# Add-and-normalise with 4 MB transfers, two rings of rows, a store lag of 48 rows, and one row in eight added on VectorE

## The chip, the core and the metric

The kernel runs on one core of one Trainium2 chip; the other cores are idle. The metric is the device time of one execution in microseconds (us). Runs of one kernel mostly agree within 0.3%. Each kernel was timed in alternating rounds with the kernel before on the same chip. A run is called fast or slow by its time and by the granted TensorE clock. "Span" is the time inside the profile, about 1.9 us shorter than the device time of the same run.

The engines are TensorE (PE in the profile; PEld is its weight load), VectorE (DVE), ScalarE (ACT) and SyncE (SP), which here only issues DMA transfers. Sixteen DMA engines move the data; every large transfer of this kernel is spread over all sixteen (sixteen landings each in the trace).

## The reference

```python
# x, residual: 16 x 1024 x 512 float32
z = x + residual
mean = np.mean(z, axis=-1, keepdims=True)
var = np.var(z, axis=-1, keepdims=True)
out = gamma * (z - mean) / np.sqrt(var + eps) + beta
```

There are 16,384 rows of 512 numbers. On 128 partitions that is 128 rows per partition, and "row" from here on means one such slice: 128 x 512 numbers, 0.26 MB. For each row the kernel loads x and the residual and stores the result, 0.79 MB; in all it moves 100.67 MB.

## The kernel before

SyncE alone issues all large transfers, in program order: the loads of a chunk, then the store of the chunk five behind.

```python
CHUNKS = [2, 2, 4] + [8] * 14 + [4, 2, 2]      # rows per chunk; 8 rows = 2 MB, 16 KB per partition
GROUP = 4                                      # rows per compute step
STORE_LAG = 5; Z_BUFS = 7; R_BUFS = 4          # in chunks

def load(c):
    z = zpool.tile(...); r = rpool.tile(...)
    nc.sync.dma_start(out=z[...], in_=rows(xf, c))
    nc.sync.dma_start(out=r[...], in_=rows(rf, c))

def g_add(g):                                  # z + r on TensorE, by an identity matrix
    for j in ...:
        nc.tensor.matmul(ps, ident, Z[c][:, j, :], start=True, stop=False)
        nc.tensor.matmul(ps, ident, R[c][:, j, :], start=False, stop=True)

# ScalarE: z <- ps with the row sum; later Square(z - mean) with its sum; sqrt
# VectorE: negmean; affine1: z <- (z - mean) * gamma; affine2: z <- z * rstd + beta
# a group's last step (affine2) comes three steps after its add

for k in range(n_chunks + STORE_LAG):
    if k < n_chunks:
        load(k)
    ...
    c = k - STORE_LAG
    if c >= 0:
        while done <= c:
            done = next(steps)
        store(c)
```

With seven z buffers and a lag of five, the x load of chunk k reuses the buffer of chunk k-7. The store of that chunk was issued after load k-2, so the loads of chunk k-1 and the store of chunk k-6 (6.3 MB) are queued between the store and the load that must wait for it.

## Time and profile before

The median is 251.63 us (251.4 to 251.81). What matters:

| Reading | Value | View |
|---|---|---|
| TensorE busy | 226.2 us, never idle from 10 to 220 us | engine totals, slices |
| VectorE, ScalarE busy | 182.7 us, 180.4 us | engine totals |
| DMA rate in steady state | 427 to 429 GB/s | windows |
| TensorE per row | 1.72 us (four matmul instructions 0.43 us apart) | timeline |
| Chain of waits | 88% TensorE | chain |

From the page of the kernel before: the engine totals, four rows of the picture in 40 slices (digits are tenths busy), and the chain of work that ended last.

```profile
PE 226.2 (91%) x516; PEld 99.2 (40%) x516; DVE 182.7 (73%) x328; ACT 180.4 (72%) x548; POOL 0.7 (0%) x6
...
PE   5999999999999999999999999999999999997000
...
DVE  1121266888888888898888888888988888889993
...
DMA  6999999999999999999999999999999999987087
GB/s 245 421 440 428 425 429 379 438 427 425 436 430 430 429 433 425 428 433 433 428 428 430 425 433 425 433 425 433 428 432 427 428 430 416 427 353 299 42 357 315
...
PE 88%; DVE 8%; DMA 1%; issue 1%; ACT 0%; DVEq 0%
```

TensorE and the DMA engines are both full until 220 us: a tuned balance. The chain names only one of them. At the end there is a hole: a slice of 42 GB/s between two of 299 and 357.

The same by windows: start and end of the window, its length, busy time of each engine, then the granted clock, the busy share of the DMA engines, and GB/s.

```profile
20.00:120.00 100.00, 100.00 (x234) 44.19 (x233) 72.27 (x129) 78.53 (x242) 0.00 (x0) 1.00 1.01 427
120.00:220.00 100.00, 100.00 (x234) 44.27 (x233) 82.59 (x148) 81.27 (x252) 0.00 (x0) 1.00 1.01 429
223.00:227.00 4.00, 4.00 (x11) 1.72 (x10) 3.77 (x8) 4.00 (x14) 0.00 (x0) 1.00 0.19 82
...
232.00:238.00 6.00, 0.00 (x0) 0.00 (x0) 5.96 (x12) 2.98 (x10) 0.00 (x0) 0.63 0.00 0
```

In the last two windows all loads are in, and the next store waits for VectorE.

Now SyncE's timeline (start, duration, line, transfer). L66 loads x, L69 the residual, L77 stores.

```profile
84.07 0.33 SPq L66 DMA_DIRECT2D z<-in_x_dram  x1
84.45 0.47 SPq L69 DMA_DIRECT2D r<-in_residual_dram  x1
88.91 0.34 SPq L77 DMA_DIRECT2D out_dram<-z  x1
98.64 0.33 SPq L66 DMA_DIRECT2D z<-in_x_dram  x1
```

The x load at 98.64 us waited for a store issued at 75.18 us. By then a load pair and another store (84.07 to 88.91) were already queued, so the DMA engines went on working. The wait list of SyncE:

```profile
SPq L66 <- DMA out_dram<-z: 135.9, 13, 13.3
```

It waited 135.9 us in 13 waits.

### The profile page before, as it was taken

The page shows a single profiled execution, that of the slowest core. Times are in us where ns is not written, and L with a number is a line of the kernel's source. Part 1 is how long each engine was busy: PE and PEld are TensorE (multiplying, and loading weights), DVE is VectorE, ACT ScalarE, POOL GpSimd, SP SyncE. Part 2 cuts the span into 40 slices and gives each one's busy share as a digit, 9 for nine tenths or more (in the row PEclk, how much of TensorE's full clock was granted, in tenths as well). Part 3 has the DMA queues.
Part 4 walks back from the last instruction along what each step waited for, and adds up shares of the span by engine and source line. Part 5 has one row for each costly group of instructions (what it writes and reads, how often), then busy time and mean ns, then how long its engine had stood idle before and what let it go on. Part 6 is the DMA issues. An engine that isn't in the chain of part 4 may idle for free.

```text
span 249.7 us, 2117 instructions
## 1 busy us (share of the span) xinstructions
PE 226.2 (91%) x516; PEld 99.2 (40%) x516; DVE 182.7 (73%) x328; ACT 180.4 (72%) x548; POOL 0.7 (0%) x6
## 2 busy tenths in 40 slices
PE   5999999999999999999999999999999999997000
PEld 1444444444444444444444444444444444442000
DVE  1121266888888888898888888888988888889993
ACT  2157578888777777788887777777888877779600
POOL 1000000000000000000000000000000000000000
PEclk9999999999999999999999999999999999999755
DMA  6999999999999999999999999999999999987087
GB/s 245 421 440 428 425 429 379 438 427 425 436 430 430 429 433 425 428 433 433 428 428 430 425 433 425 433 425 433 428 432 427 428 430 416 427 353 299 42 357 315
DMA packets 8656, 100.80 MB, mean 404 GB/s; under 512 B 962, under 2 KB 962, under 8 KB 2500
## 3 DMA queue, kind: packets, MB, share of 16 engines
q1 hardware_dynamic: 8640, 100.67, 95.4%
q8 instruction: 4, 0.07, 0.1%
q14 instruction: 8, 0.07, 0.1%
q10 hardware_dynamic: 4, 0.00, 0.0%
HBM read 67.11 MB, written 33.55 MB: 403 GB/s over the span
## 4 chain that ended last, share of the span: by engine, by line
PE 88%; DVE 8%; DMA 1%; issue 1%; ACT 0%; DVEq 0%
PE ps L112 43%; PE ps L113 43%; DVE z L191 5%; DVE z L176 3%; PE ps L98 1%; DMA gb_row<-in_gamma_dram 1%; ACT z L121 0%; DVEq L267 0%; DVE rstd L188 0%; DVE nm L163 0%
## 5 line engine op out<-in xcount | busy, mean ns | idle before, releaser
L112 PE MATMUL ps<-z,ident 128*128 128x512 f32 x256 | 132.4, 599 | 0.0
L113 PE MATMUL ps<-r,ident 128*128 128x512 f32 x256 | 131.7, 596 | 0.0
L121 ACT ACTIVATE z<-ps 128x512 f32<-128x512 f32 x128 | 75.4, 589 | 50.2 <-PE ps L113 50.2
L139 ACT ACTIVATE junk<-z,nm 128x512 f32<-128x512 f32 x128 | 90.5, 711 | 1.4 <-DVE nm L163 1.4
L191 DVE SCALAR_TENSOR_TENSOR z<-z,rstd,beta_t 128x512 f32<-128x512 f32 x128 | 87.8, 747 | 1.2
L176 DVE SCALAR_TENSOR_TENSOR z<-z,nm,gamma_t 128x512 f32<-128x512 f32 x128 | 87.7, 745 | 1.1 <-ACT junk L139 1.1
L112 PEld LDWEIGHTS ps<-z,ident 128*128 128x128 f32 x256 | 49.1, 192 | 62.8 <-issue 48.7
L113 PEld LDWEIGHTS ps<-r,ident 128*128 128x128 f32 x256 | 49.0, 192 | 62.3 <-issue 61.7
L163 DVE TENSOR_SCALAR nm<-sm 128x4 f32<-128x4 f32 (+1 forms) x34 | 5.8, 170 | 54.9 <-ACT z L121 54.9
L121 ACT ACTIVATION_READ_ACCUMULATOR z<-ps 128x1 f32 x128 | 24.9, 195 | 0.0
L139 ACT ACTIVATION_READ_ACCUMULATOR junk<-z,nm 128x1 f32 x128 | 24.4, 191 | 0.0
L151 ACT ACTIVATE std<-ssq,eps_t 128x4 f32<-128x4 f32 (+1 forms) x34 | 9.8, 289 | 0.1
L98 PE MATMUL ps<-gb_row,ones 1*128 1x512 f32 x4 | 3.7, 1085 | 3.1 <-DMA gb_row<-in_gamma_dram 3.1
L188 DVE RECIPROCAL rstd<-std 128x4 f32<-128x4 f32 (+1 forms) x34 | 5.8, 170 | 0.0
L121 ACT ACT_TABLE_LOAD x1 | 1.3, 1283 | 4.3 <-DMA z<-in_x_dram 4.3
L99 DVE COPY gamma_t<-ps 128x512 f32<-128x512 f32 x1 | 0.7, 692 | 4.2 <-PE ps L98 4.2
L98 PEld LDWEIGHTS ps<-gb_row,ones 1*128 1x128 f32 x4 | 1.1, 307 | 4.2 <-issue 3.3
L99 DVE COPY beta_t<-ps 128x512 f32<-128x512 f32 x1 | 0.7, 692 | 1.0 <-PE ps L98 1.0
L151 ACT ACT_TABLE_LOAD x1 | 1.3, 1283 | 0.0
L87 DVE MEMSET ones<- 1x128 f32 x1 | 0.2, 165 | 0.8 <-PEq L253 0.8
masks.py:199 POOL TENSOR_SCALAR_AFFINE_SELECT ident<-ident 128x128 f32<-128x128 f32 x1 | 0.3, 295 | 0.1
masks.py:197 POOL MEMSET ident<- 128x128 f32 x1 | 0.2, 205 | 0.3 <-POOLq L253 0.3
(5 smaller groups left out, 0.5 us busy)
## 6 DMA issues: line engine op xcount, KB each, us to landing
z<-in_x_dram SPq DMA_DIRECT2D x14, 2048.0 KB, 19.4
r<-in_residual_dram SPq DMA_DIRECT2D x14, 2048.0 KB, 23.9
out_dram<-z SPq DMA_DIRECT2D x14, 2048.0 KB, 26.6
z<-in_x_dram SPq DMA_DIRECT2D x4, 512.0 KB, 7.4
r<-in_residual_dram SPq DMA_DIRECT2D x4, 512.0 KB, 8.2
z<-in_x_dram SPq DMA_DIRECT2D x2, 1024.0 KB, 9.0
r<-in_residual_dram SPq DMA_DIRECT2D x2, 1024.0 KB, 15.0
out_dram<-z SPq DMA_DIRECT2D x4, 512.0 KB, 8.3
```

Of the source, the lines that this page charges most:

```text
L87: nc.vector.memset(ones, 1.0)
L98: nc.tensor.matmul(ps, ones, gb_row[:, k, :], start=True, stop=True)
L99: nc.vector.tensor_copy(dest, ps)
L112: nc.tensor.matmul(ps, ident, Z[c][:, j, :], start=True, stop=False)
L113: nc.tensor.matmul(ps, ident, R[c][:, j, :], start=False, stop=True)
L121: nc.scalar.activation(out=Z[c][:, j0 + k, :], in_=PS[g_copy][k], func=ACT.Identity, accum_out=sm[:, k : k + 1],)
L139: nc.scalar.activation(out=junk, in_=Z[c][:, j0 + k, :], func=ACT.Square, bias=NM[g_square][:, k : k + 1], accum_out=ssq[:, k : k + 1],)
L151: nc.scalar.activation(out=std[:, :n], in_=SSQ.pop(g)[:, :n], func=ACT.Sqrt, bias=eps_t[:, 0:1], scale=inv_d,)
L163: nc.vector.tensor_scalar(out=nm[:, :n], in0=NM[g][:, :n], scalar1=-inv_d, scalar2=None, op0=ALU.mult,)
L176: nc.vector.scalar_tensor_tensor(out=zj, in0=zj, scalar=NM[g][:, k : k + 1], in1=gamma_t, op0=ALU.add, op1=ALU.mult,)
L188: nc.vector.reciprocal(out=rstd[:, :n], in_=STD.pop(g)[:, :n])
L191: nc.vector.scalar_tensor_tensor(out=zj, in0=zj, scalar=rstd[:, k : k + 1], in1=beta_t, op0=ALU.mult, op1=ALU.add,)
```

## The change

Its intent: fewer, larger transfers; a deep backlog of stores, so that DMA has work while the last rows are computed; and less work on TensorE. The diff cut to its core:

```diff
-CHUNKS = [2, 2, 4] + [8] * 14 + [4, 2, 2]
+CHUNKS = [8, 8] + [16] * 6 + [8, 8]
-STORE_LAG = 5
-Z_BUFS = 7
-R_BUFS = 4
+Z_ROWS = 64
+R_ROWS = 32
+STORE_LAG = 48
+ADD_PERIOD = 8
...
+    zbuf = consts.tile([P, Z_ROWS, D], FP32)       # ring: row j lives at j % Z_ROWS
+    rbuf = consts.tile([P, R_ROWS, D], FP32)
     def load(c):
+        nc.sync.dma_start(out=part(zbuf, Z_ROWS, c), in_=rows(xf, c))
+        nc.sync.dma_start(out=part(rbuf, R_ROWS, c), in_=rows(rf, c))
...
+    def on_vector(j):
+        return j % ADD_PERIOD == ADD_PERIOD - 1
+    def add_on_vector(g): ...                      # z <- z + r with its row sum, on VectorE
...
+    for c in range(n_chunks + 1):
+        asked = end[c] if c < n_chunks else N // P + STORE_LAG
+        if c < n_chunks:
+            while added < asked - R_ROWS: ...      # residual rows must have been added
+            load(c)
+        while stored < n_chunks and end[stored] <= asked - STORE_LAG:
+            while done < end[stored]: ...
+            store(stored)
+            stored += 1
```

More of the change, by code (lines that the diff above doesn't have):

```diff
@@ L41 @@
     assert N == P * sum(CHUNKS)
-    NJ = max(CHUNKS)
-    starts = [P * sum(CHUNKS[:c]) for c in range(len(CHUNKS))]
+    first = [sum(CHUNKS[:c]) for c in range(len(CHUNKS))]
     def rows(t, c):
-        return t[starts[c] : starts[c] + P * CHUNKS[c], :].rearrange(
-            "(p j) d -> p (j d)", p=P
-        )
+        lo = P * first[c]
+        return t[lo : lo + P * CHUNKS[c], :].rearrange("(p j) d -> p (j d)", p=P)
     consts = ctx.enter_context(tc.tile_pool(name="consts", bufs=1))
-    zpool = ctx.enter_context(tc.tile_pool(name="zpool", bufs=Z_BUFS))
-    rpool = ctx.enter_context(tc.tile_pool(name="rpool", bufs=R_BUFS))
     small = ctx.enter_context(tc.tile_pool(name="small", bufs=6))
@@ L58, with part, zrow, rrow @@
     ctx.enter_context(tc.manual_schedule())
-    Z, R = {}, {}
-    def load(c):
-        n = CHUNKS[c]
-        z = zpool.tile([P, NJ, D], FP32, tag="z", name="z")
-        r = rpool.tile([P, NJ, D], FP32, tag="r", name="r")
-        nc.sync.dma_start(
-            out=z[:, :n, :].rearrange("p a b -> p (a b)"), in_=rows(xf, c)
-        )
-        nc.sync.dma_start(
-            out=r[:, :n, :].rearrange("p a b -> p (a b)"), in_=rows(rf, c)
-        )
-        Z[c], R[c] = z, r
-    def store(c):
-        n = CHUNKS[c]
-        z = Z.pop(c)
-        nc.sync.dma_start(
-            out=rows(of, c), in_=z[:, :n, :].rearrange("p a b -> p (a b)")
-        )
+    zbuf = consts.tile([P, Z_ROWS, D], FP32)
+    rbuf = consts.tile([P, R_ROWS, D], FP32)
+    def part(buf, size, c):
+        lo = first[c] % size
+        assert lo + CHUNKS[c] <= size
+        return buf[:, lo : lo + CHUNKS[c], :].rearrange("p a b -> p (a b)")
+    def load(c):
+        nc.sync.dma_start(out=part(zbuf, Z_ROWS, c), in_=rows(xf, c))
+        nc.sync.dma_start(out=part(rbuf, R_ROWS, c), in_=rows(rf, c))
+    def store(c):
+        nc.sync.dma_start(out=rows(of, c), in_=part(zbuf, Z_ROWS, c))
+    def zrow(j):
+        return zbuf[:, j % Z_ROWS, :]
+    def rrow(j):
+        return rbuf[:, j % R_ROWS, :]
+    def on_vector(j):
+        return j % ADD_PERIOD == ADD_PERIOD - 1
     gb_row = consts.tile([1, 2, D], FP32)
@@ L103, with add @@
         for j in range(0, n, GROUP):
-            groups.append((c, j, min(GROUP, n - j)))
-    PS, NM, SSQ, STD = {}, {}, {}, {}
-    def g_add(g):
-        c, j0, n = groups[g]
-        PS[g] = []
+            groups.append((first[c] + j, min(GROUP, n - j)))
+    n_groups = len(groups)
+    PS, SM, NM, SSQ, STD = {}, {}, {}, {}, {}
+    def add(g):
+        j0, n = groups[g]
+        SM[g] = small.tile([P, GROUP], FP32, tag="sm", name="sm")
         for j in range(j0, j0 + n):
+            if on_vector(j):
+                continue
@@ L111, in g_add @@
             ps = psum.tile([P, D], FP32, tag="ps", name="ps")
-            nc.tensor.matmul(ps, ident, Z[c][:, j, :], start=True, stop=False)
-            nc.tensor.matmul(ps, ident, R[c][:, j, :], start=False, stop=True)
-            PS[g].append(ps)
-    def act_step(g_copy, g_square, g_sqrt):
-        if g_copy is not None:
-            c, j0, n = groups[g_copy]
-            sm = small.tile([P, GROUP], FP32, tag="sm", name="sm")
-            for k in range(n):
+            nc.tensor.matmul(ps, ident, zrow(j), start=True, stop=False)
@@ new lines, in add, with add_on_vector @@
+            nc.tensor.matmul(ps, ident, rrow(j), start=False, stop=True)
+            PS[j] = ps
+    def add_on_vector(g):
+        j0, n = groups[g]
+        for j in range(j0, j0 + n):
+            if on_vector(j):
+                nc.vector.scalar_tensor_tensor(
+                    out=zrow(j),
+                    in0=zrow(j),
+                    scalar=0.0,
+                    in1=rrow(j),
+                    op0=ALU.add,
+                    op1=ALU.add,
+                    accum_out=SM[g][:, j - j0 : j - j0 + 1],
+                )
@@ L121, in act_step, with copy @@
+    def copy(g):
+        j0, n = groups[g]
+        for j in range(j0, j0 + n):
+            if j in PS:
                 nc.scalar.activation(
-                    out=Z[c][:, j0 + k, :],
-                    in_=PS[g_copy][k],
+                    out=zrow(j),
+                    in_=PS.pop(j),
                     func=ACT.Identity,
-                    accum_out=sm[:, k : k + 1],
+                    accum_out=SM[g][:, j - j0 : j - j0 + 1],
                 )
-                if k == 0 and g_sqrt is not None:
-                    sqrt(g_sqrt)
-                    g_sqrt = None
@@ L130, in act_step, with negmean @@
-            NM[g_copy] = sm
-            PS.pop(g_copy)
-        if g_sqrt is not None:
-            sqrt(g_sqrt)
-        if g_square is not None:
-            c, j0, n = groups[g_square]
-            ssq = small.tile([P, GROUP], FP32, tag="ssq", name="ssq")
-            for k in range(n):
-                junk = junkp.tile([P, D], FP32, tag="junk", name="junk")
-                nc.scalar.activation(
-                    out=junk,
-                    in_=Z[c][:, j0 + k, :],
-                    func=ACT.Square,
-                    bias=NM[g_square][:, k : k + 1],
-                    accum_out=ssq[:, k : k + 1],
-                )
-            SSQ[g_square] = ssq
+    def negmean(g):
+        n = groups[g][1]
+        nm = small.tile([P, GROUP], FP32, tag="nm", name="nm")
+        nc.vector.tensor_scalar(
+            out=nm[:, :n],
+            in0=SM.pop(g)[:, :n],
+            scalar1=-inv_d,
+            scalar2=None,
+            op0=ALU.mult,
+        )
+        NM[g] = nm
@@ L148, in sqrt, with square @@
+    def square(g):
+        j0, n = groups[g]
+        ssq = small.tile([P, GROUP], FP32, tag="ssq", name="ssq")
+        for k in range(n):
+            junk = junkp.tile([P, D], FP32, tag="junk", name="junk")
+            nc.scalar.activation(
+                out=junk,
+                in_=zrow(j0 + k),
+                func=ACT.Square,
+                bias=NM[g][:, k : k + 1],
+                accum_out=ssq[:, k : k + 1],
+            )
+        SSQ[g] = ssq
     def sqrt(g):
-        n = groups[g][2]
+        n = groups[g][1]
@@ L158, in sqrt @@
         STD[g] = std
-    def negmean(g):
-        n = groups[g][2]
-        nm = small.tile([P, GROUP], FP32, tag="nm", name="nm")
-        nc.vector.tensor_scalar(
-            out=nm[:, :n],
-            in0=NM[g][:, :n],
-            scalar1=-inv_d,
-            scalar2=None,
-            op0=ALU.mult,
-        )
-        NM[g] = nm
     def affine1(g):
-        c, j0, n = groups[g]
+        j0, n = groups[g]
         for k in range(n):
-            zj = Z[c][:, j0 + k, :]
             nc.vector.scalar_tensor_tensor(
-                out=zj,
-                in0=zj,
+                out=zrow(j0 + k),
+                in0=zrow(j0 + k),
                 scalar=NM[g][:, k : k + 1],
@@ L183, in affine1 @@
             )
+        NM.pop(g)
     def affine2(g):
-        c, j0, n = groups[g]
+        j0, n = groups[g]
         rstd = small.tile([P, GROUP], FP32, tag="rstd", name="rstd")
@@ L189, in affine2 @@
         for k in range(n):
-            zj = Z[c][:, j0 + k, :]
             nc.vector.scalar_tensor_tensor(
-                out=zj,
-                in0=zj,
+                out=zrow(j0 + k),
+                in0=zrow(j0 + k),
                 scalar=rstd[:, k : k + 1],
@@ L198, in affine2 @@
             )
-        NM.pop(g)
-    n_groups = len(groups)
-    def ok(g):
-        return g if 0 <= g < n_groups else None
     def compute_steps():
-        done = 0
-        for t in range(n_groups + 3):
-            if ok(t) is not None:
-                g_add(t)
-            act_step(ok(t), ok(t - 1), ok(t - 2))
-            if ok(t - 2) is not None:
-                affine1(t - 2)
-            if ok(t) is not None:
-                negmean(t)
-            if ok(t - 3) is not None:
-                affine2(t - 3)
-                c, j0, n = groups[t - 3]
-                if j0 + n == CHUNKS[c]:
-                    done = c + 1
-            yield done
+        stages = [
+            (0, add),
+            (0, add_on_vector),
+            (0, copy),
+            (2, sqrt),
+            (1, square),
+            (2, affine1),
+            (0, negmean),
+            (3, affine2),
+        ]
+        added = done = 0
+        for t in range(n_groups + 3):
+            for lag, stage in stages:
+                if 0 <= t - lag < n_groups:
+                    stage(t - lag)
+            if t < n_groups:
+                added += groups[t][1]
+            if t >= 3:
+                done += groups[t - 3][1]
+            yield added, done
     steps = compute_steps()
-    done = 0
+    added = done = stored = 0
     n_chunks = len(CHUNKS)
-    for k in range(n_chunks + STORE_LAG):
-        if k < n_chunks:
-            load(k)
-        if k == 0:
-            spread()
-        c = k - STORE_LAG
-        if c >= 0:
-            while done <= c:
-                done = next(steps)
-            store(c)
+    end = [first[c] + CHUNKS[c] for c in range(n_chunks)]
+    for c in range(n_chunks + 1):
+        asked = end[c] if c < n_chunks else N // P + STORE_LAG
+        if c < n_chunks:
+            while added < asked - R_ROWS:
+                added, done = next(steps)
+            assert stored == n_chunks or first[stored] >= asked - Z_ROWS
+            load(c)
+        if c == 0:
+            spread()
+        while stored < n_chunks and end[stored] <= asked - STORE_LAG:
+            while done < end[stored]:
+                added, done = next(steps)
+            store(stored)
+            stored += 1
 _INS = ['x', 'residual', 'gamma', 'beta', 'eps']
```

## The prediction

> **What bounds the kernel now.** Two things, so evenly that neither waits in steady state. Table by stage (20 us stretches from 20 to 220 us): the 16 DMA engines are busy all the time and move 416 to 431 GB/s; the kernel must move 100.67 MB, so about 234 us at 430. That is near the 435 GB/s ceiling in the Trainium skill ("DMA: Bandwidth & Descriptors", Specifications). TensorE is busy in every one of these stretches as well: 226 us of 250, matmul starts 0.43 us apart, 4 per row, 1.72 us a row; the chain of waits lies 86% on it.
>
> DMA's loss beyond 234 us is at the ends. Start: no bytes before 1.6 us, then 307 to 389 GB/s until 8 us with the small chunks. End: stores wait for compute: the 40 slices show 353, 299, 42, 357, 315 GB/s, and SyncE waits 29 us for VectorE after 220 us. Against 430 GB/s that is about 11 us lost.
>
> **What the change does.**
> 1. One row in eight leaves TensorE: 1.72 x 7/8 = 1.50 us a row. VectorE gets 16 more passes of about 0.75 us: 183 to about 195 us, also 1.5 a row. Compute can now keep ahead of DMA (1.83 us a row at 430 GB/s).
> 2. Stores 48 rows behind: when the last load lands, about 12.6 MB of stores (29 us) remain, enough to cover the last rows' compute. The 11 us hole at the end should go.
> 3. 16 and 32 KB lines from the start: about 1 us at the start and at most 1 to 1.5 us in steady state, as 430 is near the ceiling.
> 4. New cost: z ring 64 rows minus lag 48 leaves 16 rows, exactly one chunk. In SyncE's order the x loads of chunks 5, 6, 7 and 8 each wait for completion of the store issued immediately before them, with nothing queued behind. DMA runs dry four times. Before, 6 MB always lay in between. Estimated cost of a hole: about 0.6 us from the last byte to the semaphore (end of the profile), 0.9 us from issue to the first packet and about 0.5 us ramp (start of the profile) = 2.0 us; the skill's fixed cost of about 2 us per DMA ("DMA: Bandwidth & Descriptors", Anatomy of one DMA) agrees. Four holes: 8 us, plus 0.8 us for unequal engines (the drain at 223 to 226 us shows up to 3 us of skew).
>
> **Sum.** Start 2.1 + transfer 233.1 + holes 8.8 + end 1.4 = 245.4 us span; plus 1.9 us (time over span before) = 247.3 us. The holes give back most of the tail's gain.
>
> **What would show each step.** DMA about 430 GB/s up to the end including a store-only last 30 us; four dips of about 2 us in fine windows (near 90, 121, 154 and 186 us), each ended by an x load; SyncE's wait "x load on store" remaining, its last waits on VectorE nearly gone; TensorE near 200 us busy; the chain of waits moving from TensorE to DMA.
>
> **What would make it wrong.** Holes nearer 1 us, or 32 KB lines giving 435: about 243. Holes over 3 us, slower store-only or load-only streams, or the residual load of chunk 4 waiting for TensorE (I find only about 4 us slack): 250 or more.
>
> Predicted 247.3 us, 8 in 10 between 244.3 and 250.6; faster by over 2%: 0.36, within 2%: 0.60, slower: 0.04.

## The result, and the profile after

The changed kernel is correct and slower: median 261.99 us (261.9 to 262.05) against 251.63. The ratio is 1.041, 95% interval 1.039 to 1.043. (A ratio is the mean time of one kernel's fast runs over that of the other's of the same rounds, so it is not quite the ratio of the medians.)

The same lines of the page as before:

```profile
PE 207.9 (80%) x452; PEld 89.3 (34%) x452; DVE 191.0 (73%) x356; ACT 169.9 (65%) x514; POOL 0.7 (0%) x6
...
PE   3699996999999999998998069993699999990000
...
DVE  1101438399999999999799803999319999999980
...
DMA  7999999999999869999399997899959999999957
GB/s 257 431 441 463 423 408 473 407 418 449 418 433 405 376 247 408 466 332 463 106 409 460 342 433 272 363 463 403 390 257 332 433 433 400 418 451 423 410 249 322
...
DMA 49%; PE 37%; DVE 8%; SPq 1%; issue 1%; ACT 0%; DVEq 0%
```

TensorE was relieved as intended (226.2 to 207.9 us busy), and the chain moved from TensorE to DMA. But four slices now fall to 247, 106, 272 and 257 GB/s, and TensorE has gaps of its own behind them.

SyncE's timeline (here L69 loads x, L70 the residual, L73 stores) shows a new pattern: each x load is preceded by silence, and nothing is queued between the store and the load.

```profile
92.76 0.34 SPq L69 DMA_DIRECT2D zbuf<-in_x_dram  x1
93.20 0.37 SPq L70 DMA_DIRECT2D rbuf<-in_residual_dram  x1
93.62 0.42 SPq L73 DMA_DIRECT2D out_dram<-zbuf  x1
127.78 0.33 SPq L69 DMA_DIRECT2D zbuf<-in_x_dram  x1
```

The load at 127.78 us overwrites the rows of the store issued at 93.62 us. Ring (64) minus lag (48) leaves 16 rows, which is one chunk. The total of this wait is smaller than before, and yet here it costs:

```profile
SPq L69 <- DMA out_dram<-zbuf: 121.9, 4, 33.7
```

The windows around the four x loads, columns as before:

```profile
90.00:94.00 4.00, 4.00 (x11) 1.76 (x10) 3.96 (x10) 3.69 (x14) 0.00 (x0) 1.00 0.46 133
124.00:129.00 5.00, 5.00 (x13) 2.17 (x12) 3.85 (x9) 4.61 (x14) 0.00 (x0) 1.00 0.32 92
159.00:163.00 4.00, 4.00 (x11) 1.77 (x10) 2.32 (x6) 3.08 (x10) 0.00 (x0) 1.00 0.46 131
193.00:197.00 4.00, 4.00 (x11) 1.77 (x10) 2.96 (x7) 3.72 (x12) 0.00 (x0) 1.00 0.39 82
```

One cycle, from one x load to the next, moves 12.58 MB: 24 packets of 32 KB for each DMA engine. A packet takes 1.213 us when nothing disturbs it, so 24 take 29.1 us. The cycles took 35.0, 33.6 and 33.5 us:

```profile
92.76:127.78 35.02, 33.57 (x79) 14.70 (x78) 32.64 (x62) 28.78 (x88) 0.00 (x0) 1.00 0.89 360
127.78:161.38 33.60, 24.27 (x53) 10.44 (x52) 21.67 (x42) 19.04 (x60) 0.00 (x0) 0.85 0.92 375
161.38:194.92 33.54, 27.16 (x58) 11.69 (x57) 23.79 (x45) 21.15 (x67) 0.00 (x0) 0.90 0.92 376
```

So a dry spell costs 4.4 to 5.9 us and not the 2.2 us that the prediction had put on it (2.0, and a quarter of 0.8 for unequal engines). The semaphore and packet records of the trace show why (landings of the store on the 16 engines, issue of the x load that waits for it):

```
store lands on its first .. last engine   spread   x load issued
 90.60 ..  92.70                           2.10       92.76
124.70 .. 127.77                           3.07      127.78
159.74 .. 161.36                           1.62      161.38
193.33 .. 194.91                           1.58      194.92
```

SyncE reacts at once (0.01 to 0.06 us). It waits for the slowest of 16 engines, though, while the others are idle already. After the issue nearly a microsecond passes before the first packets, and those packets are slow: from 160 to 164 us they took 1.86 us on average instead of 1.21. Packets were slow again where each of these cycles turns from the residual load to the store (180 to 184 us: 1.55 us on average). Per dry spell, no engine had a packet for 1.3 to 1.45 us, close to the 1.5 us that the prediction had for semaphore and issue together. Before that, engines that had finished waited for the slowest: 1.1 to 2.6 us per spell, averaged over the sixteen, and 6.6 us in all four, where the prediction had 0.8.

The end of the kernel has a second problem. The residual of chunk 7 (rows 96 to 111) landed at 184.25 us, with 32 rows still to be added. From there:

```profile
184.30:234.40 50.10, 50.10 (x110) 21.82 (x110) 39.94 (x77) 38.01 (x117) 0.00 (x0) 0.95 0.95 395
234.40:251.00 16.60, 0.04 (x1) 0.00 (x0) 16.46 (x29) 7.11 (x21) 0.00 (x0) 0.59 0.97 418
251.00:254.00 3.00, 0.00 (x0) 0.00 (x0) 2.16 (x4) 0.00 (x0) 0.00 (x0) 0.50 0.05 22
254.00:259.00 5.00, 0.00 (x0) 0.00 (x0) 0.00 (x0) 0.00 (x0) 0.00 (x0) 0.50 0.99 419
```

TensorE needs 50.1 us for 32 rows (1.57 us each). VectorE ends at 253.2 us, 18.8 us behind TensorE, and the last store, 2 MB, is issued then and lands 6.3 us later. That is 76 us from the landing to the end. For most of it the DMA engines still had stores and loads to move, so only the last few us of this tail were time that DMA lost.

### The profile page after: what moved, and what is told of

It is laid out like the page before. It is cut to its first block, busy times and chain, and to the rows that moved or that the text cites. A ratio compares the mean times of both kernels' runs of the same rounds, so it can differ in the third digit from the quotient of the medians.

```text
span 260.3 us, 1971 instructions
## 1 busy us (share of the span) xinstructions
PE 207.9 (80%) x452; PEld 89.3 (34%) x452; DVE 191.0 (73%) x356; ACT 169.9 (65%) x514; POOL 0.7 (0%) x6
## 4 chain that ended last, share of the span: by engine, by line
DMA 49%; PE 37%; DVE 8%; SPq 1%; issue 1%; ACT 0%; DVEq 0%
DMA out_dram<-zbuf 26%; DMA rbuf<-in_residual_dram 24%; PE ps L119 19%; PE ps L118 18%; DVE zbuf L203 5%; DVE zbuf L188 3%; SPq L69 1%; SPq L70 1%; ACT zbuf L140 0%; DVEq L285 0%; DVE zbuf L126 0%; DVE rstd L201 0%; DVE nm L150 0%
## 5 line engine op out<-in xcount | busy, mean ns | idle before, releaser
L119 PE MATMUL ps<-rbuf,ident 128*128 128x512 f32 x224 | 120.6, 621 | 21.6 <-DMA rbuf<-in_residual_dram 21.6
L118 PE MATMUL ps<-zbuf,ident 128*128 128x512 f32 x224 | 119.3, 615 | 0.0
L140 ACT ACTIVATE zbuf<-ps 128x512 f32<-128x512 f32 x112 | 65.7, 588 | 63.1 <-PE ps L119 63.1
L164 ACT ACTIVATE junk<-zbuf,nm 128x512 f32<-128x512 f32 x128 | 90.4, 709 | 0.0
L188 DVE SCALAR_TENSOR_TENSOR zbuf<-zbuf,nm,gamma_t 128x512 f32<-128x512 f32 x128 | 87.8, 746 | 2.1 <-ACT junk L164 2.1
L203 DVE SCALAR_TENSOR_TENSOR zbuf<-zbuf,rstd,beta_t 128x512 f32<-128x512 f32 x128 | 87.7, 747 | 1.1
L119 PEld LDWEIGHTS ps<-rbuf,ident 128*128 128x128 f32 x224 | 43.9, 198 | 80.0 <-issue 53.5
L118 PEld LDWEIGHTS ps<-zbuf,ident 128*128 128x128 f32 x224 | 44.4, 199 | 57.9 <-issue 45.6
L164 ACT ACTIVATION_READ_ACCUMULATOR junk<-zbuf,nm 128x1 f32 x128 | 24.2, 189 | 0.0
L140 ACT ACTIVATION_READ_ACCUMULATOR zbuf<-ps 128x1 f32 x112 | 21.7, 194 | 0.0
## 6 DMA issues: line engine op xcount, KB each, us to landing
zbuf<-in_x_dram SPq DMA_DIRECT2D x6, 4096.0 KB, 12.5
```

What stands on the lines that cost most here:

```text
L118: nc.tensor.matmul(ps, ident, zrow(j), start=True, stop=False)
L119: nc.tensor.matmul(ps, ident, rrow(j), start=False, stop=True)
L140: nc.scalar.activation(out=zrow(j), in_=PS.pop(j), func=ACT.Identity, accum_out=SM[g][:, j - j0 : j - j0 + 1],)
L164: nc.scalar.activation(out=junk, in_=zrow(j0 + k), func=ACT.Square, bias=NM[g][:, k : k + 1], accum_out=ssq[:, k : k + 1],)
L188: nc.vector.scalar_tensor_tensor(out=zrow(j0 + k), in0=zrow(j0 + k), scalar=NM[g][:, k : k + 1], in1=gamma_t, op0=ALU.add, op1=ALU.mult,)
L203: nc.vector.scalar_tensor_tensor(out=zrow(j0 + k), in0=zrow(j0 + k), scalar=rstd[:, k : k + 1], in1=beta_t, op0=ALU.mult, op1=ALU.add,)
```

## The experiments

**Theory A**: the x load now waits for the store issued just before it; DMA runs dry four times, which delays the last landings, and behind them stands a compute tail. **Rival B**: 4 MB transfers and 32 KB lines are slow in themselves. **Rival C**: the add on VectorE slows the compute pipeline. All kernels gave correct results.

### Residual first

```diff
     def load(c):
-        nc.sync.dma_start(out=part(zbuf, Z_ROWS, c), in_=rows(xf, c))
+        if c < 5:
+            nc.sync.dma_start(out=part(zbuf, Z_ROWS, c), in_=rows(xf, c))
         nc.sync.dma_start(out=part(rbuf, R_ROWS, c), in_=rows(rf, c))
+        if c >= 5:
+            nc.sync.dma_start(out=part(zbuf, Z_ROWS, c), in_=rows(xf, c))
```

> From chunk 5 on, the residual load (which waits for nothing recent) is issued ahead of the x load; nothing else changes. Theory A (the x load waits for the store just queued, DMA runs dry, each cycle of 12.6 MB takes 33.5 to 35 us instead of 29.1): the four dry stretches at 92, 127, 161 and 194 us vanish, the cycle falls to 29.1 to 30 us, the loads of chunk 7 have landed by 168 to 172 us instead of 184, and the time falls to 247 to 250 us, since from that landing to the end the profile shows 76 us of compute and last store that this edit leaves alone. Rival B (the 32 KB lines and 4 MB transfers are themselves slow): cycles stay near 33 us and the time stays within 2 us of 262. Rival C (compute with the vector add is what is slow): also 260 to 262.

Measured: 249.45 us in the profiled run, and 252.98, 253.03 and 253.22 us in the other three (the last counted as slow); ratio to the kernel before 1.002 (0.994 to 1.009). So it gains 9 to 12.5 us over the changed kernel by swapping two instructions. Only the profiled run lies in the expected 247 to 250 us; the median missed it by 3 us. SyncE's timeline (L71 residual, L73 x, L76 store):

```profile
114.06 0.33 SPq L71 DMA_DIRECT2D rbuf<-in_residual_dram  x1
124.82 0.33 SPq L73 DMA_DIRECT2D zbuf<-in_x_dram  x1
```

The three cycles, by windows, columns as before:

```profile
92.84:124.82 31.98, 30.81 (x73) 13.51 (x72) 29.97 (x57) 26.04 (x82) 0.00 (x0) 1.00 1.02 423
124.82:153.90 29.08, 24.25 (x54) 10.54 (x53) 22.03 (x42) 19.35 (x61) 0.00 (x0) 0.94 1.00 431
153.90:182.97 29.07, 25.85 (x61) 11.20 (x60) 25.14 (x49) 22.53 (x69) 0.00 (x0) 1.00 0.99 425
```

The x load still waits for the store, but 4 MB of residual are queued behind that store. Two of the three cycles fall to 29.1 us at the same transfer size; the first took 32.0 us at 423 GB/s. The loads of chunk 7 have landed by 173.2 us, a little later than expected, and the span ends 74 us later. That is A, and against B. Three of four runs lay 3.5 us above the profiled one, with a granted clock of 0.925 to 0.933 against 0.950; no trace of those was taken, so this stays open.

### All chunks of eight rows

```diff
-CHUNKS = [8, 8] + [16] * 6 + [8, 8]
+CHUNKS = [8] * 16
```

> All chunks 8 rows (2 MB transfers, 16 KB lines); rings and lag of 48 unchanged. The 16 rows between ring and lag are now two chunks, so a load pair and a store stand between a store and the x load that waits for it. Theory A: no dry stretches, and the last compute starts from a load of 8 rows instead of 16, so 243 to 248 us. Rival B (large transfers slow): also faster, so this run alone does not tell A from B; with the residual-first run it does: if both are fast, A. Rival C (compute): 258 or more.

Measured: 246.10 us (245.98 to 247.58; the profiled run is the slowest of the four); ratio 0.980 (0.978 to 0.984). It is faster than the kernel before, but the interval doesn't settle whether by 2%. Sixteen rows are now two chunks, the dry spells are gone, and the rate is 424 to 437 GB/s in every slice from 6 to 220 us. The holes at the end stay: the slices there read 251, 211 and 260 GB/s.

```profile
GB/s 249 432 432 437 429 429 427 425 425 424 429 432 427 429 431 427 427 437 427 432 425 425 432 429 432 432 429 435 427 432 425 428 429 432 427 429 408 251 211 260
```

### The kernel before with six z buffers

```diff
-Z_BUFS = 7
+Z_BUFS = 6
```

> The kernel before with six z buffers instead of seven, lag still five: now each x load waits for the store issued just before it, with 2 MB transfers and no vector add. Theory A: a dry stretch of 3.5 to 5.5 us per chunk of 6.3 MB, about 13 to 15 of them, so 295 to 325 us. Rival B or C: the old kernel's transfers and compute are unchanged, so at most a few us over 251.6.

Measured: 294.67 us (293.75 to 295.32); ratio 1.173. This is the same fault put into the old kernel, with 2 MB transfers and no vector add. SyncE's timeline there:

```profile
129.73 0.33 SPq L66 DMA_DIRECT2D z<-in_x_dram  x1
130.11 0.42 SPq L69 DMA_DIRECT2D r<-in_residual_dram  x1
130.62 0.38 SPq L77 DMA_DIRECT2D out_dram<-z  x1
147.94 0.33 SPq L66 DMA_DIRECT2D z<-in_x_dram  x1
```

A cycle of 6.3 MB (24 packets of 16 KB for each engine) took 18.0 to 19.2 us in the middle of the run instead of 14.6, so a dry spell cost 3.4 to 4.6 us. The total, 43 us, falls just short of the 295 us at the lower edge of the expectation; it is far outside what B and C allowed.

### The kernel before with the vector add

```diff
     def g_add(g):
         ...
         for j in range(j0, j0 + n):
+            if on_vector(c, j):          # one row in eight
+                PS[g].append(None)
+                continue
...
+                add_on_vector(t)         # VectorE, right after the group's matmuls
```

> The kernel before with one row in eight added on VectorE, transfers and buffers unchanged. Theory A: TensorE 1.5 us a row, compute keeps ahead of DMA, the hole of about 11 us in the stores at the end shrinks by half or more: 241 to 247 us. Rival C (the vector add slows the compute pipeline): 251 to 260 us.

Measured: 245.47 us (244.47 to 247.57); ratio 0.978 (0.972 to 0.983). The vector add alone makes the old kernel 2.2% faster, although the interval doesn't settle whether by more than 2%. C falls. The gain is at the end, as the windows of this run show; the two holes of the kernel before, about 3 us and 6 us of idle DMA, have become one of about 4.3 us:

```profile
223.00:228.00 5.00, 0.15 (x1) 0.00 (x0) 4.96 (x12) 3.89 (x13) 0.00 (x0) 0.74 0.98 419
228.00:233.00 5.00, 0.00 (x0) 0.00 (x0) 4.96 (x11) 1.81 (x5) 0.00 (x0) 0.50 0.14 59
```

### The changed kernel without the vector add

```diff
     def on_vector(j):
-        return j % ADD_PERIOD == ADD_PERIOD - 1
+        return False
```

> The changed kernel with every add back on TensorE, all else kept (4 MB transfers, rings, lag 48). Theory A: the dry stretches stay, and the 32 rows after the landing of chunk 7 take 1.72 us a row instead of 1.57, with a landing some 3 us later since the residual loads also wait for TensorE: 266 to 274 us. Rival C (vector add is what made it slower): 262 or less.

Measured: 269.03 us (268.37 to 269.31); ratio 1.069. The vector add was worth 7 us inside the changed kernel as well. The landing came only 1.5 us later (185.8 us), less than expected; then 32 rows took TensorE 56 us.

### Stores 32 rows behind

```diff
-STORE_LAG = 48
+STORE_LAG = 32
```

> Stores 32 rows behind instead of 48, all else as in the changed kernel: a load pair and a store lie between a store and the x load that waits for it. Theory A: no dry stretches, but more stores go ahead of the last loads, so chunk 7 lands at 177 to 181 us (184 in the changed kernel, 173 with the residual first) and about 75 us of compute and last store follow: 252 to 258 us. Rival B (4 MB transfers slow): 260 or more.

Measured: 260.57 us (258.82 to 262.29); ratio 1.036. The time missed the expectation of A by 2.6 us, and by itself would fit B. The trace separates the two. No x load waited for a store any more, and from the residual of chunk 5 to that of chunk 7 the cycles took 29.0 and 30.2 us with 4 MB transfers, which speaks against B. But the residual of chunk 7 landed at 184.4 us, as in the changed kernel, and not at the expected 177 to 181. I had counted that more stores go ahead of the loads, but not that the first stores were now asked for before their rows were ready, so that SyncE stood until 66.4 us on a store and held the next loads back. That this explains the whole delay is argued, not tested. The smaller backlog then left DMA idle while the last rows were computed:

```profile
219.00:233.00 14.00, 14.00 (x34) 6.08 (x32) 13.78 (x27) 12.35 (x40) 0.00 (x0) 1.00 0.14 59
```

### The changed kernel with a small last chunk

```diff
-CHUNKS = [8, 8] + [16] * 6 + [8, 8]
+CHUNKS = [8, 8] + [16] * 6 + [8, 4, 2, 2]
```

> The changed kernel with only its last chunk of 8 rows cut into 4, 2 and 2; the four dry stretches stay. Theory A says that the end is the compute chain behind the landing of chunk 7, so the landing stays at 184 us, the last store shrinks from 6.3 to about 2.7 us and the pipeline drain by 1 to 2 us: 255 to 259 us. If DMA were what ends last, the same bytes would end at the same time: 261 to 263.

Measured: 260.82 us (259.56 to 261.18); ratio 1.036. I had expected 255 to 259. The landing stayed at 184.8 us, so the dry spells were as before, but only 1.2 us were won. DMA moved 392 GB/s from 245 us until 257 us, with VectorE at work for only 8.7 of these 12 us: chunk 7's store, 4 MB, cannot start before its sixteenth row is done (233.5 us), the next store follows at 245.3 us, and that work now ends last.

```profile
245.00:257.00 12.00, 0.00 (x0) 0.00 (x0) 8.68 (x16) 0.00 (x0) 0.00 (x0) 0.50 0.94 392
```

In the changed kernel the compute tail and DMA's own backlog end within some 2 us of each other. So the dry spells are the main cause, and the compute tail a second one just behind them.

### The old chunks in the new rings

```diff
-CHUNKS = [8, 8] + [16] * 6 + [8, 8]
+CHUNKS = [2, 2, 4] + [8] * 14 + [4, 2, 2]
```

> The changed kernel with the old kernel's chunks (2, 2, 4, fourteen of 8, then 4, 2, 2): rings, lag of 48 and vector add kept. Against the run with chunks of 8: the last load and the last store are of 2 rows instead of 8, so the last store costs about 2.7 us instead of 6.3, and compute after the last landing is short. Theory A: 239.5 to 243.5 us, faster than every kernel so far; the end bounded by DMA or within 3 us of it. If the compute pipeline is instead behind by more than the last landing: 245 to 247, as with chunks of 8.

Measured: 245.38 us (244.47 to 246.45); ratio 0.976. Above the expected 239.5 to 243.5: all sixteen DMA engines had data almost without a break from 2 to 238 us, and the last one ended at 242.2 us, so DMA itself was the bound. The expectation had not counted the slowest engine's delay and the cost of small transfers. The run also clears the rings and the lag of 48 as such: with the old chunks they are faster than the kernel before.

### Eights with a small last chunk

```diff
-CHUNKS = [8, 8] + [16] * 6 + [8, 8]
+CHUNKS = [8] * 15 + [4, 2, 2]
```

> Chunks of 8 rows throughout, only the last one cut into 4, 2 and 2; rings, lag 48 and vector add kept. The run with small chunks at both ends was bound by DMA to the last store: its engines were never idle together between 2 and 239 us, but the slowest of the 16 finished 4 us after the mean, and its slices from 67 to 91 us, where small stores go out, moved 394 to 417 GB/s. Theory A: leaving out the small chunks at the start gains 0.5 to 2 us: 243 to 245 us. If compute sets the end after all: 245.5 to 246.5, as with chunks of 8.

Measured: 243.24 us (243.03 to 243.42) in five rounds, as expected; ratio 0.967 (0.966 to 0.969). This is the fastest kernel, 3.3% faster than the kernel before and 7% below the changed one. Its slices have no hole at all:

```profile
DMA  7999999999999999999999999999999999999994
GB/s 248 435 424 435 429 429 432 420 433 426 424 429 426 429 431 432 426 432 424 429 433 429 431 426 435 429 429 429 424 435 428 422 416 432 429 426 432 435 414 185
```

### All kernels in one account

The packet records of the traces allow the same sum for every kernel. The 100.66 MB are 384 packets of 16 KB per DMA engine; at 0.607 us, the time from one packet's start to the next when nothing disturbs them, that is 233.1 us. "Idle" counts, at every moment, how many packets fewer than sixteen are under way, and divides the sum by sixteen; "slow" is what packets took beyond 0.607 us per 16 KB. The three add up to 0.7 to 1.5 us more than the span, because the records of successive packets overlap by some nanoseconds. Idle, slow and span are those of the profiled run.

| Kernel | Idle | Slow | Span | Median time |
|---|---|---|---|---|
| before | 13.5 | 4.6 | 249.7 | 251.6 |
| changed | 19.4 | 8.5 | 260.3 | 262.0 |
| changed, residual first | 10.4 | 4.8 | 247.5 | 253.0 |
| changed, chunks of 8 | 10.6 | 3.3 | 245.8 | 246.1 |
| before, six z buffers | 35.9 | 24.4 | 291.9 | 294.7 |
| before, vector add | 8.5 | 4.5 | 244.6 | 245.5 |
| changed, lag 32 | 22.7 | 4.2 | 259.3 | 260.6 |
| changed, small last chunk | 18.0 | 8.7 | 258.9 | 260.8 |
| changed, no vector add | 24.2 | 10.0 | 266.6 | 269.0 |
| changed, old chunks | 6.6 | 5.3 | 243.5 | 245.4 |
| eights, small last chunk | 5.6 | 3.9 | 241.3 | 243.2 |

Two things can be read off. Slow packets of 8 us and more occur only in the kernels with dry spells; with 4 MB transfers and no dry spells (residual first, lag 32) they are as few as with 2 MB. And since all kernels move the same bytes, every gain must show here as idle or slow time of DMA taken away; the table says which.

## Why the prediction was wrong, point by point

- **What bounds the kernel before: right.** DMA and TensorE are both full, and the loss is at the ends. The vector add alone took back 6 us of it.
- **Step 1, TensorE relieved: right.** 207.9 us busy against the "near 200" that I expected, since TensorE ran at half its clock after some stalls (below); VectorE has 191.0 us against 195.
- **Step 2, the store backlog covers the last compute ("The 11 us hole at the end should go"): only in part.** It assumed that compute is close behind the loads. It was 32 rows behind when chunk 7 landed at 184.25 us, and needed 50.1 us for them, 18.8 us to drain, and 6.3 us for a last store of 2 MB. DMA's idle time after 200 us fell from 10.9 us in the kernel before to 4.2 us, of which 2.8 us lie around the wait for VectorE at 251 to 254 us. The dry spells hid part of the miss, because they held DMA back while compute caught up: with the residual first and no dry spells the idle time after 200 us is 7.3 us. With dry spells gone and a small last chunk the backlog did cover it: 3.3 us idle, 243.24 us.
- **Step 3, larger lines: right that it is small.** An undisturbed 32 KB packet took 1.213 us and two of 16 KB 1.222 us; from start to start it is 1.209 against 1.214. Over 192 packets that is 1.0 to 1.7 us, near the 1 to 1.5 us predicted for steady state, and no run shows it in the time. The predicted 1 us at the start did not come: the first 10 us moved 317 instead of 307 GB/s, which is about 0.2 us.
- **Step 4, four dry spells at the places named (90, 121, 154, 186 us; seen near 92, 127, 161 and 194): right in the mechanism, and mis-sized.** This is the step that failed most, and in it the term for unequal engines. I put 2.0 us on each hole and 0.8 us on unequal engines for all four together. In the trace the store's landing is spread over 1.6 to 3.1 us at every one of them, which cost 6.6 us of idle in place of 0.8, and packets are slow after each restart and at the turn to the store, which I had at most as a ramp of 0.5 us. Swapping two instructions removed the holes and 9 to 12.5 us. The sum also took every packet at its best, while kernels without dry spells lose 3 to 5 us to slow packets.

The sum, in us of span:

| Term | Predicted | Measured |
|---|---|---|
| start | 2.1 | 2.1 |
| packets at their best | 233.1 | 233.1 |
| four dry spells, idle | 8.8 | 12.8 |
| slow packets | 0, but for the ramp in the 8.8 | 8.5, of which 3 to 5 are there in kernels without dry spells too |
| end | 1.4 | 4.1 (2.8 around the wait for VectorE, 1.3 after the last packets) |
| other idle, less overlap in the records | 0 | 0.5 - 0.7 |
| span | 245.4 | 260.3 |

The measured terms are rounded and add up to within 0.1 us of the span.

Two citations can be checked. The Trainium skill, "DMA: Bandwidth & Descriptors", Specifications, gives 435 GB/s as the ceiling; the trace agrees with 427 to 431 GB/s in steady state. Its section Anatomy of one DMA gives a fixed cost of about 2 us per transfer, but for transfers issued through GpSimd, and here SyncE issues them. So it is no evidence for my 2.0 us for a dry queue (the clause that called on it is cut from the prediction above). In these runs a dry queue cost 3.4 to 5.9 us, and the measurement decides.

"TensorE: Matmul & The Clock Gate", Part 1, says that the clock is halved after at least one idle window of about 3.4 us and restored after at least one busy window of that length. The trace agrees in part. After a wait of 6.38 us that ended at 184.29 us, the first matmul pair took 2.08 us instead of 1.02 us, and the granted clock from 180 to 190 us averaged 0.66:

```profile
176.89 1.02 PE L118 MATMUL ps<-zbuf,ident 128*128 128x512 f32 x2
184.29 2.08 PE L119 MATMUL ps<-rbuf,ident 128*128 128x512 f32 x2 [6.38 <-DMA rbuf<-in_residual_dram]
```

The half-clock stretches while TensorE still had work lasted 3.4, 10.2 and 6.8 us, which are one, three and two such windows. But the first of them, from 42.9 to 46.4 us, followed a wait of only 2.10 us (40.46 to 42.57 us), and in the residual-first run a wait of 3.22 us before 173.38 us was followed by none. A stall of DMA can thus be paid for once more on TensorE; what that added to the time was not tested.

## What to carry to other kernels

When transfers are issued in order, ask of every wait what is queued behind the transfer that it waits for: a wait of 136 us in total cost nothing with 6 MB queued, and the waits with nothing queued cost 3.4 to 5.9 us each. A ring's size minus the lag should therefore be at least two chunks, or an instruction that need not wait must be issued first; enlarging the chunk without the ring can take the slack away unnoticed. A deep store backlog pays only if compute keeps close behind the loads, which calls for small last chunks.

## What the Trainium skill lacked or had wrong

- "DMA: Bandwidth & Descriptors" has no figure for letting the queue run dry when SyncE issues the transfers: here 4.4 to 5.9 us per dry spell with 4 MB transfers and 3.4 to 4.6 us with 2 MB. With 4 MB it is made of the engines' unequal finish (landings spread over 1.6 to 3.1 us), the restart (nearly 1 us) and slow packets afterwards (1.86 us on average instead of 1.21).
- The same page, section Where 436 GB/s comes from, says that for HBM to SBUF transfers the HBM side (about 358 GB/s) binds. On this core, with the others idle, loads and stores together ran at 427 to 431 GB/s. The page "HBM Reference", Specifications, gives about 425 GB/s for a core that streams alone, and the runs agree with that.
- The same page's rule of at least 1 MiB per transfer has no upper end. From 16 KB to 32 KB per partition under 1% was gained (1.222 us for two packets of 16 KB, 1.213 for one of 32 KB), and going from 2 to 4 MB halves how many transfers fit in the same ring.
- "TensorE: Matmul & The Clock Gate", Part 1, asks for an idle window of about 3.4 us before the clock is halved. Here a wait of 2.10 us was followed by half a clock for 3.4 us, and one of 3.22 us in another run was not.
- No page tells what sets the engines' unequal finish when SyncE issues the transfers. In the run with all chunks of eight rows the spread of a load's landings grew from 0.8 us (landing at 42 us) to 2.3 us (at 54 us), while two packets of the instruction queues, of 0.31 and 1.10 us, ran at 46.6 and 47.7 us. Whether they caused it was not tested.
